# gMLP u products: where the fetches of v, the modulation steps, the first mixing and one PSUM copy stand in the queues

## The chip, the cores and the metric

One core of one Trainium2 chip runs the whole program. The metric is the device time of one execution in microseconds (us), given as the median of several runs. The engines of the core work from queues of their own, in order: PE (TensorE, matmuls, with its weight loads listed as PEld), DVE (VectorE), ACT (ScalarE), POOL (GpSimd, which also issues some transfers) and SP (which only issues transfers). Each waits on semaphores for what another engine or a transfer has finished.

## The reference

Two layers of a hybrid backbone work on 512 latent tokens and 256 context tokens of width 1024, in float32. Each layer is FFN, token mixer, FFN; each part is modulated by vectors made from a conditioning vector and closed by a LayerNorm. The first layer's mixer is the gated MLP that this change touches:

```python
def modulation(cond, w_mod, b_mod):
    m = jax.nn.silu(cond) @ w_mod + b_mod
    return jnp.split(m[..., None, :], N_MOD, axis=-1)

def gmlp_mix(h, w_in, sgu_g, sgu_b, w_s, b_s, w_out):
    b_, t_, _ = h.shape
    u, v = jnp.split(jax.nn.gelu(h @ w_in, approximate=False), 2, axis=-1)
    v = layer_norm(v, sgu_g, sgu_b)
    v = v.reshape(b_, t_ // CHUNK, CHUNK, GMLP_GROUPS, GMLP_HALF // GMLP_GROUPS)
    v = jnp.einsum('gpq,bnqgc->bnpgc', w_s, v) + b_s.T[None, None, :, :, None]
    return (u * v.reshape(b_, t_, GMLP_HALF)) @ w_out
```

u and v are 3072 wide. v is normalised over its width, mixed over each chunk of 128 tokens by a 128x128 matrix per group (8 groups of 384 columns), multiplied with u, and projected back to 1024.

## The kernel before

Every float32 product is made of three fp32r products: an operand is split into a rounded part (a CAST on ACT) and the rest (a subtraction on DVE), and of the four products the smallest is left out. All recorded engine instructions pass through one helper, so most rows name line 90.

**The u products.** `gmlp` (line 1426) first makes v, all of which is written to DRAM (`v_spill`), and then runs a loop over 24 column blocks j of u, two per turn, a = 0, 2, ..., 22. A turn holds seven Strassen products of 12 matmuls, named B11, T1, T2, B21, T3, B22, T4, each over 384 tokens (half of the 768). They share three kinds of PSUM banks: `seeded` (takes a copy of B11's result, then T2, T3 and T4 on top), `b1` (B11, then B21 on top) and `b2` (T1, then B22 on top). Because T3 adds to the bank in which T2's result still has to be read, the copy of T2's bank to SBUF must be done before T3 starts; the bank of T1 in the next turn must have been read by the addition after B22.

**A slot.** After each product `step` (line 1537) calls `slot` (line 181), which writes instructions in this order: the subtractions of the splits that are due (`flush`), an `early` function if one is given, up to two new weight units (`pump`: CASTs on ACT, sums for Strassen on DVE, loads into 6 `raw` buffers on SP as these come free; 8 `w` buffers hold finished units), modulation steps if `fills` is set, and then `post`: the reading of the bank, and up to two pieces of the list `late`. A pass of the program's own scheduling then sets the final order on DVE and ACT; PE, SP and POOL keep the order in which they were written.

**The mixing.** `spatial(j)` (line 1500) multiplies the six normalised 128x128 blocks of v's column block j with the group's matrix into two of four mixing banks that are used in turn. A transposition and a small product of the next group take one bank of the four every third j. `mixed(0)` and `mixed(1)` read the two banks on DVE (three 128-wide blocks each, into `S`), and `times` multiplies `S` with u into `stage`, which POOL writes to DRAM. `fetch(j + 4)` asks SP for the block of v that goes into the ring place that j has just left. For a > 0, `spatial(a)` stands between B21 and T3 and `spatial(a+1)` between B22 and T4; the turn a = 0 does both after T4.

**Modulation steps.** `fill` runs one step of `mod_unit` (line 453): two DVE multiply-adds of a loaded 128x512 piece of w_mod (`mraw`, 3 buffers, loaded on SP) into `acc`; every eighth step ends with two all-reduces over partitions on POOL (line 476) and the next begins with two TENSOR_SCALARs. This sub-layer has 48 steps: 33 in the u loop (T1, B21 and B22 of a = 2 to 20, and T4 of a = 4, 12 and 20), 13 in the first half of the output projection, 2 in its second half.

**The output projection.** `out_proj` (line 884) reads the products back through POOL transfers into `q`, splits them and multiplies them with 24 weight pieces per half of the 1024 columns. In the first seven slots of the second half the six banks of the first half are added to z, one per slot.

Of the kernel before, what the change touches and what calls it, by code (L numbers as in the profile page):

```python
# [94 lines left out]
class Backbone:  # L95
# [788 lines left out]
    def out_proj(self, acts, l, i, factor, end, prev, gate_at=2):  # L884

        self.pin(True)
        n = acts.n
        orders = acts.order
        acts.feed(0, 3)
        self.new_z(NB)  # L890
        residual = []
        st = self.stats(NB)
        banks, adds = {}, []
        for half, order in enumerate(orders):
            body = n - CLOSE * half
            for x in range(body):
                f = order[x]
                (w,) = self.weights(1)
                for b in range(NB):
                    if not x:  # L900
                        if half:
                            z = self.z[b][:, 0:512]
                            adds.append((b, z, self.gated(b, 0, banks[b], factor)))
                            self.unhold(("out", b))
                        banks[b] = self.bank(("out", b))
                    self.products(banks[b], b, [acts.of(f)], [w], x == 0, x == n - 1)
                    if b == 2:
                        self.flush()
                        self.pump(1)
                        acts.prepare(half, x + AHEAD)  # L910
                self.release(1)
                self.flush()
                if not half and x == 1:
                    residual = self.residual(prev, NB)
                if not half and x == gate_at:
                    self.load_gate(l, i + 2, NB)
                if not half or x > 3:
                    acts.feed(half, 3 - half)
                if adds:
                    if x:  # L920
                        b, z, tmp = adds.pop(0)
                        self.dve.tensor_tensor(z, z, tmp, ALU.add)
                        self.dve.bn_stats(st[b][:, 0], z)
                    self.fill(int(prev is None or self.light))
                elif residual and x > 2 and (half or x % 2):
                    residual.pop(0)()
                    self.fill(int(self.light))
                elif half or x < n - 1:
                    self.fill_pair()
                    if prev is None and x % 8 == 3:  # L930
                        self.fill()
        assert not residual
        rest = [acts.of(f) for f in orders[1][n - CLOSE :]]
        ws = self.weights(CLOSE)
        self.flush()
        self.pump()
        self.pin(False)

        def closing(b, between):
            self.products(banks[b], b, rest[:2], ws[:2], False, False)  # L940
            turned = between()
            self.products(banks[b], b, rest[2:], ws[2:], False)
            if b == NB - 1:
                self.release(CLOSE)
                self.pump(1 if end.strassen else 9)

            def add():
                self.add_gated(b, 1, banks[b], factor, st[b])
                self.unhold(("out", b))

            return [add], st[b], turned

        end.run(NB, closing)
# [472 lines left out]
    def gmlp(self, l, i, nblocks, end, prev):  # L1426
# [45 lines left out]
        def fetch(j):  # L1472
            if j < GMLP_CH:
                src = spill[j // 4][:, (j % 4) * P : (j % 4) * P + P].rearrange("(b p) c -> p b c", p=P)
                self.sp.dma_start(ring[:, j % 4], src)
# [18 lines left out]
            dve.scalar_tensor_tensor(nb, mv[:, :, 0], -1.0, self.v_rs, ALU.mult, ALU.mult)  # L1494

        self.following = group(0)
        late = []
        kept = {}

        def spatial(j):  # L1500
            if j % 3 == 0:
                self.grp = self.grp_next
                self.following = group(j // 3 + 1) if j // 3 + 1 < GMLP_GROUPS else iter((None, None, None))
            wT, r, bs = self.grp
            self.grp_next = next(self.following)
            if j % 3 == 2:
                load_ws(j // 3 + 2)
            v = ring[:, j % 4]
            banks = [mix_bank(), mix_bank()]
            for b in range(NB):  # L1510
                o = (b % HALF) * P
                self.mm(banks[b // HALF][:, o : o + P], v[:, b], wT, True, True)
            fetch(j + 4)
            box = []

            def mixed(x):
                if not x:
                    base = self.sm([P], "base", 2)
                    sc = self.sguT[:, GMLP_CH + j : GMLP_CH + j + 1]
                    dve.scalar_tensor_tensor(base, r, sc, bs, ALU.mult, ALU.add)  # L1520
                    box.append(base[:, :].unsqueeze(1).to_broadcast([P, HALF, P]))
                cut = lambda t: t.rearrange("p (b t) -> p b t", t=P)
                out = cut(S[j % 2][:, x * HT : x * HT + HT])
                gain = self.sguT[:, j : j + 1]
                dve.scalar_tensor_tensor(out, cut(banks[x][:, 0:HT]), gain, box[0], ALU.mult, ALU.add)

            late.extend([lambda: mixed(0), lambda: mixed(1)])
# [9 lines left out]
        def step(ps, name, go_on, early, *posts, fills=0):  # L1537
            self.product(ps, name, go_on)

            def post():  # L1540
                for f in posts:
                    f()
                for _ in range(2):
                    if late:
                        late.pop(0)()

            self.slot(post, 2, fills, early)
            self.release(1)

        add = lambda out, a, b: dve.tensor_tensor(out, a, b, ALU.add)  # L1550
# [7 lines left out]
        for a in range(0, GMLP_CH, 2):  # L1558
            begin, final = not a, a == GMLP_CH - 2
            seeded = self.part_bank("mixed", marked=True)  # L1560
            b1, extra = self.part_bank(), int(not begin and a < GMLP_CH - 2)
            step(b1, "B11", False, lambda: act.copy(seeded, b1), v_stats if begin else lambda: normed(a))
            b2, p5 = self.part_bank(), temp()
            step(b2, "T1", False, None, lambda: act.copy(p5, b2), v_bias if begin else nothing, fills=extra)
            if begin:
                next(self.following)
            if final:
                acts.prepare(0, 0)
                acts.feed(0, 1)
            v = temp()  # L1570
            half = (lambda j, x: lambda: normed(j, range(HALF * x, HALF * x + HALF))) if begin else lambda j, x: nothing
            step(seeded, "T2", True, None, lambda: act.copy(v, seeded), half(0, 0))
            g = temp()
            step(b1, "B21", True, None, lambda: gelu(g, b1), half(0, 1), fills=extra)
            if begin:
                self.grp_next = next(self.following)
            else:
                spatial(a)
                late.append(lambda a=a, g=g: times(a, T1, g))
            w = temp()  # L1580
            step(seeded, "T3", True, lambda: act.copy(w, seeded), half(1, 0) if begin else lambda: normed(a + 1))
            if final:
                acts.prepare(0, 1)
                acts.feed(0, 1)
            step(b2, "B22", True, None, lambda: add(v, v, b2), lambda: add(w, w, p5), half(1, 1), fills=extra)
            if begin:
                self.filler_raw()
            else:
                spatial(a + 1)
            if a == GMLP_CH - 4:  # L1590
                acts.feed(0, 1)
            x = temp()

            def last():
                gelu(v, v)
                gelu(w, w)
                gelu(x, seeded)

            step(seeded, "T4", True, None, last, fills=int(extra and a % 8 == 4))
            self.unhold("mixed")  # L1600
            if final:
                acts.prepare(0, 2)
            if begin:
                spatial(a)
                late.append(lambda a=a, g=g: times(a, T1, g))
                late.append(lambda a=a, v=v: times(a, T2, v))
                spatial(a + 1)
            else:
                late.append(lambda a=a, v=v: times(a, T2, v))
            late.append(lambda a=a, x=x: times(a + 1, T1, x))  # L1610
            late.append(lambda a=a, w=w: times(a + 1, T2, w))
# [734 lines left out]
```

## Time and profile before

| what | value |
|---|---|
| median of 3 runs | 2789.63 us (2788.86 to 2789.99) |
| the profiled execution | 2794.73 us, of which the span is 2792.9 us |
| u loop and mixing | from 736.4 us to 966.2 us of the span |
| output projection | from 966.2 us to about 1169 us |
| PE busy over the span | 2735.2 us (98%) |
| mean granted TensorE clock | 0.994 |

The page lists busy times by engine and by group of instructions; the span is from the first to the last instruction of the profiled execution. A timeline row holds a start, a duration, the engine, the operation and, in brackets, how long the engine sat idle before it and what ended that. In a row of windows the number after the engines' busy times is the clock that the throttle granted to PE in that stretch, 1.00 being full speed. SPq rows are transfers issued by SP. A merged row (x6) covers several instructions.

### The profile page before, as it was taken

Reading aid. Unit: us, or ns where it says so; the run is one execution under the profiler, and the core shown is the slowest. Engines: PE = TensorE matmul, PEld = TensorE weight load, DVE = VectorE, ACT = ScalarE, POOL = GpSimd, SP = SyncE. Lnnn points to the kernel's source line nnn. Section 1 sums busy time; section 2 is a strip of 40 time slices with the busy share of each in tenths; the row PEclk is TensorE's granted clock in tenths of the full one; section 3 lists DMA queues with packets and bytes.
Section 4 is the critical chain, followed back from the end, with each engine's and each line's share of the span. In section 5 each row is a group of like instructions: output and inputs, shape, how many; then the busy total and the mean of one; then the engine's idle time right before and its main releaser. Section 6 shows DMA issues by size and latency. Waiting matters only on the chain.

```text
span 2792.9 us, 40728 instructions
## 1 busy us (share of the span) xinstructions
PE 2735.2 (98%) x14234; PEld 2464.5 (88%) x14234; DVE 2085.0 (75%) x3554; ACT 1313.8 (47%) x2624; POOL 554.2 (20%) x627
## 2 busy tenths in 40 slices
PE   7999999999999999999999999999999999999998
PEld 5999987887899988899998889999888888888887
DVE  6879979586789876587898659789796698733445
ACT  6544432475656632564444246444432666623321
POOL 1002144212123231200314120013242121000001
PEclk9999999999999999999999999999999999999999
DMA  7445466367666683444456534454594424454352
GB/s 234 134 140 144 142 225 213 110 212 226 201 187 184 190 271 105 132 147 147 136 147 224 169 105 146 139 151 137 174 309 147 147 72 90 132 149 130 111 170 87
DMA packets 408134, 448.09 MB, mean 160 GB/s; under 512 B 29624, under 2 KB 289144, under 8 KB 407928
## 3 DMA queue, kind: packets, MB, share of 16 engines
q1 hardware_dynamic: 371416, 331.99, 38.5%
q0 software_dynamic: 36512, 113.51, 13.4%
q8 instruction: 111, 1.82, 0.3%
q14 instruction: 95, 0.78, 0.1%
HBM read 383.40 MB, written 64.19 MB: 160 GB/s over the span
## 4 chain that ended last, share of the span: by engine, by line
PE 58%; DVE 2%; ACT 2%; issue 2%; POOL 1%; DMA 1%; SPq 0%; DVEq 0%; POOLq 0%; ACTq 0%
PE ps L90 57%; PE pp L90 1%; POOL acc L476 1%; ACT h L694 0%; ACT z L2244 0%; POOL rs L204 0%; ACT p L1758 0%; DMA mraw<-in_w_mod_dram 0%; DMA q<-act 0%; DVE z L90 0%; DVE nm L1750 0%; DVE w L90 0%; ACT w L173 0%; ACT comb L708 0%; DVE q L90 0%
## 5 line engine op out<-in xcount | busy, mean ns | idle before, releaser
L90 PE MATMUL ps<-comb,w 128*128 128x384 f32 x6552 | 1155.4, 336 | 11.7 <-ACT q L90 4.4
L90 PEld LDWEIGHTS ps<-comb,w 128*128 128x128 f32 x6552 | 1139.5, 189 | 17.1 <-ACT q L90 5.5
L90 PE MATMUL ps<-w,acts 128*128 128x512 f32 (+1 forms) x3792 | 864.8, 390 | 7.1 <-DVE q L90 5.1
L90 PEld LDWEIGHTS ps<-w,acts 128*128 128x128 f32 x3792 | 709.2, 188 | 154.6 <-DVE q L90 6.0
L90 ACT CAST w<-raw 128x512 fp32r<-128x512 f32 x643 | 397.8, 622 | 638.9 <-PE ps L90 547.6
L90 DVE TENSOR_TENSOR w<-raw,w 128x512 fp32r<-128x512 f32 x643 | 476.8, 746 | 291.1 <-ACT w L90 289.7
L90 DVE SCALAR_TENSOR_TENSOR acc<-mraw,cs,acc 128x512 f32<-128x512 f32 x392 | 279.8, 745 | 26.2 <-DMA mraw<-in_w_mod_dram 25.9
L476 POOL PARTITION_ALL_REDUCE acc<-acc x56 | 206.5, 3693 | 326.8 <-DVE acc L90 306.6
L90 PE MATMUL ps<-h,w 128*128 128x512 f32 (+1 forms) x1152 | 241.4, 372 | 0.2 <-DVE w L174 0.2
L90 PEld LDWEIGHTS ps<-h,w 128*128 128x128 f32 x1152 | 203.3, 188 | 37.7 <-DVE w L174 0.4
L90 POOL DMA_DIRECT2D act<-stage x86 | 49.7, 578 | 878.1 <-DVE stage L90 791.7
L90 POOL DMA_DIRECT2D q<-act x234 | 132.4, 603 | 450.8 <-DVE acts L90 276.7
L90 ACT COPY q<-ps 128x384 f32<-128x384 f32 (+1 forms) x218 | 104.7, 480 | 228.2 <-PE ps L90 228.1
L90 DVE TENSOR_TENSOR w<-sums,w 128x512 fp32r<-128x512 f32 x234 | 166.9, 721 | 45.6 <-ACT w L90 45.4
L90 PE MATMUL ps<-w,comb 128*128 128x512 f32 x756 | 173.7, 390 | 2.5 <-ACT ps L90 2.0
L90 ACT CAST w<-sums 128x512 fp32r<-128x512 f32 x234 | 144.9, 620 | 64.1 <-DVE sums L339 39.2
L90 PEld LDWEIGHTS ps<-w,comb 128*128 128x128 f32 x756 | 141.3, 188 | 33.5 <-ACT ps L90 2.9
L90 ACT CAST acts<-q 128x384 fp32r<-128x384 f32 (+1 forms) x272 | 131.9, 519 | 66.9 <-DMA q<-act 48.8
L90 DVE TENSOR_TENSOR acts<-q,acts 128x384 fp32r<-128x384 f32 (+1 forms) x272 | 153.7, 602 | 12.2 <-ACT acts L90 12.2
L204 POOL TENSOR_TENSOR rs<-ve,mhalf 128x1 f32<-128x1 f32 (+3 forms) x47 | 38.6, 820 | 273.6 <-DVE ve L201 170.7
L90 DVE TENSOR_TENSOR q<-q,ps 128x384 f32<-128x384 f32 (+1 forms) x81 | 46.1, 570 | 57.7 <-PE ps L90 57.6
L174 DVE TENSOR_TENSOR w<-raw,w 128x512 fp32r<-128x512 f32 x101 | 67.2, 688 | 25.6 <-ACT w L173 25.1
(203 smaller groups left out, 2484.3 us busy)
## 6 DMA issues: line engine op xcount, KB each, us to landing
raw<-in_ffn_w_in_dram SPq DMA_DIRECT2D x400, 256.0 KB
mraw<-in_w_mod_dram SPq DMA_DIRECT2D x256, 256.0 KB
raw<-in_ffn_w_out_dram SPq DMA_DIRECT2D x176, 256.0 KB
q<-act POOLq DMA_DIRECT2D x224, 192.0 KB, 4.3
raw<-in_gmlp_w_in_dram SPq DMA_DIRECT2D x132, 256.0 KB
act<-stage POOLq DMA_DIRECT2D x76, 384.0 KB, 3.2
zhat<-z POOLq DMA_DIRECT2D x26, 512.0 KB, 3.0
raw<-in_gmlp_w_out_dram SPq DMA_DIRECT2D x48, 256.0 KB
```

The costliest lines, as they stand in the source:

```text
L90: return self.tc.keep_in_program_order(f(*args, **kwargs))
L174: self.lows.append((key, lambda: self.dve.tensor_tensor(lo, src, hi.bitcast(F32), ALU.subtract)))
L204: self.last_rstd = self.nc.gpsimd.tensor_tensor(rs, ve, self.mhalf[:, 0:1].to_broadcast([P, n]), ALU.pow).ins
L476: nc.gpsimd.partition_all_reduce(accs[c], accs[c], P, bass_isa.ReduceOp.add)
```

## The change

Five edits, all in the mixer of the first layer:

1. `fetch(j + 4)` is no longer issued at once by `spatial(j)`. It goes on a list with a counter of 2, which every later `step` lowers, and is issued at the end of the second one.
2. Modulation steps in the u loop start at a = 4 and leave T4 out: 27 in place of 33 (T1, B21 and B22 of a = 4 to 20). `step` hands 0 to `slot` and calls `fill_pair` itself, behind `post` and behind the fetches. The first three loads of `mraw` move from a = 0 to the end of B22 of a = 2. In the output projection of this mixer (`acts.ring`), the seven slots at the start of the second half run a step each, which they did not before.
3. T2's copy out of `seeded` becomes the slot's `early` function, written ahead of the weight CASTs.
4. In the turn a = 0, the two `mixed` of j = 0 are called as soon as `spatial(0)` is written, not two slots later.
5. The conditions around these are rewritten to fit.

```diff
@@ out_proj
-                    self.fill(int(prev is None or self.light))
+                    self.fill(int(prev is None or self.light or acts.ring))
@@ gmlp
-        late = []
+        late, fetches = [], []
...
-            fetch(j + 4)
+            fetches.append([2, j + 4])
...
-            self.slot(post, 2, fills, early)
+            self.slot(post, 2, 0, early)
+            for x in fetches:
+                x[0] -= 1
+            while fetches and fetches[0][0] <= 0:
+                fetch(fetches.pop(0)[1])
+            if fills:
+                self.fill_pair()
             self.release(1)
...
-            b1, extra = self.part_bank(), int(not begin and a < GMLP_CH - 2)
+            b1, extra = self.part_bank(), int(3 < a < GMLP_CH - 2)
...
-            step(seeded, "T2", True, None, lambda: act.copy(v, seeded), half(0, 0))
+            step(seeded, "T2", True, lambda: act.copy(v, seeded), half(0, 0))
...
-            if begin:
+            if not begin:
+                spatial(a + 1)
+            if a == 2:
                 self.filler_raw()
-            else:
-                spatial(a + 1)
...
-            step(seeded, "T4", True, None, last, fills=int(extra and a % 8 == 4))
+            step(seeded, "T4", True, None, last, fills=0)
...
             if begin:
                 spatial(a)
+                for _ in range(2):
+                    late.pop(0)()
                 late.append(lambda a=a, g=g: times(a, T1, g))
```

On ACT, in the slots of T1, T2 and B21 of one turn (the last six blocks of v normalised, then `w<-sums` and `w<-raw` as weight CASTs, `q<-ps` as copies out of PSUM, the last row being the gelu after B21):

```order
 L90 ACTIVATE v<-v,v_nb,rs_7221 128x128 x6
 L90 CAST w<-sums 128x512
-L90 COPY q<-ps 128x384
-L90 CAST w<-sums 128x512
-L90 COPY q<-ps 128x384
+L90 COPY q<-ps 128x384 x2
+L90 CAST w<-sums 128x512
 L90 CAST w<-raw 128x512
 L90 ACTIVATE q<-ps 128x384
```

The second copy, which is T2's, now follows T1's copy directly, and the second CAST of a sum has gone behind it; this holds in the turns a = 2 to 20 (in a = 22 two CASTs of the output projection's first operand stand between the copies).

On DVE, at the end of the turn a = 0, with the numbers of the buffers (`ps_7369` of before and `ps_7363` of the change are the first mixing bank of j = 0, `S_7185` the mixed result, `s512` the row that is added to it). Before:

```order
L90 TENSOR_TENSOR w_7332<-sums_7239,w_7332 128x512
L339 TENSOR_TENSOR sums_7435<-sums_7434,raw_7126 128x512
L90 TENSOR_TENSOR w_7361<-raw_7106,w_7361 128x512
L90 SCALAR_TENSOR_TENSOR s512_7415<-S_7185,sguT_82 128x128
L90 TENSOR_SCALAR acc_7442<-mraw_7341,cs_78 128x512
L90 SCALAR_TENSOR_TENSOR S_7185<-ps_7369,sguT_82,s512_7415 128x384
```

and with the change:

```order
L90 TENSOR_TENSOR w_7332<-sums_7239,w_7332 128x512
L90 SCALAR_TENSOR_TENSOR s512_7371<-S_7185,sguT_82 128x128
L90 SCALAR_TENSOR_TENSOR s512_7436<-S_7185,sguT_82 128x128
L339 TENSOR_TENSOR sums_7431<-sums_7430,raw_7126 128x512
L90 SCALAR_TENSOR_TENSOR S_7185<-ps_7363,sguT_82,s512_7371 128x384
```

Between the same subtraction for a weight and the reading of the first mixing bank there were four operations, one of them a modulation step's; now there are three, two of them 128 wide.

On POOL, from the turn a = 18 to the last (`act<-stage` are the products written to DRAM, L476 the all-reduces of modulation, L477 their transfers, `q<-act` the first product read back for the output projection):

```order
 L90 DMA act_18_7181<-stage 128x768
 L90 DMA act_19_7182<-stage 128x768
-L476 ISA acc<-acc 128x512
-L477 DMA mod_8467<-acc 16x1x32
-L476 ISA acc<-acc 128x512
-L477 DMA mod_8467<-acc 16x1x32
 L90 DMA q<-act_0_7163 128x384 x2
-L90 DMA mod_9427<-in_b_mod_dram 16x64 x2
 L90 DMA act_20_7183<-stage 128x768
 L90 DMA act_21_7184<-stage 128x768
```

A pair of all-reduces that stood ahead of the first reading back has left this place. Over the u loop POOL had four such pairs and now has three.

## The prediction

> **What bounds the kernel now.** The page first:
>
> ```profile
> span 2792.9 us, 40728 instructions
> PE 2735.2 (98%) x14234; PEld 2464.5 (88%) x14234; DVE 2085.0 (75%) x3554; ACT 1313.8 (47%) x2624; POOL 554.2 (20%) x627
> PE 58%; DVE 2%; ACT 2%; issue 2%; POOL 1%; DMA 1%; SPq 0%; DVEq 0%; POOLq 0%; ACTq 0%
> ```
>
> PE is busy for 98% of the span and leads the chain of waits, so edits that leave the matmuls alone can only win where PE stands still. The PE timeline of the u loop shows where (start, duration, in brackets the idle time ahead and what ended it):
>
> ```profile
> 756.84 1.62 PE L90 MATMUL ps<-zraw,v 128*128 128x128 f32 x6 [3.22 <-DVE S L90]
> 811.07 0.91 PE L90 MATMUL ps<-zraw,v 128*128 128x128 f32 x6 [0.96 <-DVE S L90]
> 817.92 8.09 PE L90 MATMUL ps<-comb,w 128*128 128x384 f32 x36 [1.76 <-DVE q L90]
> 864.08 4.43 PE L90 MATMUL ps<-comb,w 128*128 128x384 f32 x24 [0.81 <-ACT q L90]
> 883.64 4.43 PE L90 MATMUL ps<-comb,w 128*128 128x384 f32 x24 [1.27 <-ACT q L90]
> 903.62 4.46 PE L90 MATMUL ps<-comb,w 128*128 128x384 f32 x24 [1.80 <-ACT q L90]
> 958.03 4.45 PE L90 MATMUL ps<-comb,w 128*128 128x384 f32 x24 [0.51 <-ACT q L90]
> 970.49 36.60 PE L90 MATMUL ps<-w,acts 128*128 128x512 f32 x153 [2.02 <-ACT q L90]
> ```
>
> Eight gaps, 12.35 us. Three cost more than their length. The windows right behind the first, third and last, and for contrast behind the sixth (third figure from the end: granted clock):
>
> ```profile
> 756.00:761.00 5.00, 4.16 (x17) 4.19 (x18) 3.95 (x9) 0.00 (x0) 0.57 (x1) 0.66 0.76 212
> 818.00:822.00 4.00, 4.00 (x14) 4.00 (x15) 4.00 (x9) 4.00 (x10) 0.00 (x0) 0.57 0.35 95
> 971.00:976.00 5.00, 5.00 (x16) 3.93 (x16) 5.00 (x11) 2.84 (x6) 2.43 (x5) 0.66 0.51 151
> 903.00:908.00 5.00, 4.38 (x25) 4.38 (x26) 5.00 (x11) 3.55 (x10) 1.18 (x2) 1.00 0.51 158
> ```
>
> A window of 5 us at 0.66 loses 5 x 0.34 = 1.7 us of matmul time, one of 4 us at 0.57 4 x 0.43 = 1.7. So three gaps have a clock loss of 1.7 us each behind them, and 12.35 + 5.1 = 17.5 us is all that can be won here, 0.6% of the span.
>
> **First mixing (edit 4): 3.6 us.** In the turn a = 0 `spatial(1)` needs, for its second bank, the bank of `mixed(0)` of j = 0. DVE before that gap:
>
> ```profile
> 752.39 0.68 DVE L90 TENSOR_TENSOR w<-sums,w 128x512 fp32r<-128x512 f32 x1
> 753.11 0.69 DVE L339 TENSOR_TENSOR sums<-sums,raw 128x512 f32<-128x512 f32 x1
> 754.32 0.34 DVE L90 SCALAR_TENSOR_TENSOR s<-S,sguT 128x128 f32<-128x128 f32 x1
> 755.68 0.49 DVE L90 TENSOR_SCALAR acc<-mraw,cs 128x512 f32<-128x512 f32 x1 [1.02 <-DMA mraw<-in_w_mod_dram]
> 756.08 1.14 DVE L90 SCALAR_TENSOR_TENSOR S<-ps,sguT,s 128x384 f32<-128x384 f32 x2
> ```
>
> A modulation step with a late `mraw` stands in front of the reading (756.08, the first of two 0.57 long; PE goes on at 756.84). In the new order the same subtraction is followed by two 128-wide operations, L339 and then the reading: 752.39 + 0.6 + 2 x 0.3 + 0.65 = 754.2 as its start (each start follows the last by a little less than its duration), its end at 754.8, PE on at 755.0. PE stopped at 753.62 (756.84 - 3.22), so 1.3 us of gap stay and 1.9 go. If nothing came of it 0, if all went 3.2. I also count the 1.7 of clock, because gaps of 1.27 and 1.80 us above had x24 at full rate behind them (4.43 and 4.46 us): 3.6. It is not sure, since length alone doesn't decide: 1.76 us lost the clock, 1.80 did not (rival 1).
>
> [...]
>
> **T2's copy (edit 3): 4.4 us.** The four gaps that end with "ACT q" ahead of x24 stand in front of T3. One of them, at 903.62:
>
> ```profile
> 898.98 3.49 POOL L476 PARTITION_ALL_REDUCE acc<-acc  x1
> 899.19 2.69 DVE L90 TENSOR_TENSOR stage<-q,S 128x384 f32<-128x384 f32 x1
> 901.80 0.68 DVE L339 TENSOR_TENSOR sums<-sums,raw 128x512 f32<-128x512 f32 x1
> 902.57 0.62 ACT L90 CAST w<-sums 128x512 fp32r<-128x512 f32 x1 [4.20 <-DVE sums L339]
> 903.09 0.47 ACT L90 COPY q<-ps 128x384 f32<-128x384 f32 x1
> ```
>
> ACT stood 4.20 us for the sum, with T2's copy behind it. The copy now goes first; T2 ends one product (about 2.1 us, 12 of the x24 in 4.43) and a spatial ahead of T3, and the copy takes 0.47, so it is covered. Behind it now wait the CAST of the sum and, through it, B21's gelu and T3's copy; the weights are several slots ahead, and T3's copy has the length of B22 and a spatial, some 4 us, as cover. All four go: 0.81 + 1.27 + 1.80 + 0.51 = 4.39; from below 0, if the next ACT wait takes their place.
>
> **Fewer steps, behind the slot's work (edit 2): 4.4 us at a = 6.** What led to the second and third gap:
>
> ```profile
> 802.79 5.87 POOL L476 PARTITION_ALL_REDUCE acc<-acc  x1
> 805.48 3.45 DVE L90 TENSOR_SCALAR acc<-mraw,cs 128x512 f32<-128x512 f32 x2
> 810.29 3.48 SPq L90 DMA_DIRECT2D raw<-in_gmlp_w_in_dram  x3
> 816.71 0.69 DVE L336 TENSOR_TENSOR sums<-raw 128x512 f32<-128x512 f32 x1 [3.33 <-DMA raw<-in_gmlp_w_in_dram]
> 817.32 0.55 DVE L90 TENSOR_TENSOR q<-q,ps 128x384 f32<-128x384 f32 x1
> ```
>
> While an all-reduce runs, a DVE operation that comes in its later part is held (3.45 us here for two that take 0.5 each, 2.69 for one of 0.55 above). Here the pair of all-reduces was issued by step 8 in T1 of a = 6 and step 9 ran into it. That made the mixing late (0.96), then SP's loads, then L336, behind which the addition waited that frees T1's bank (1.76, and 1.7 of clock). Counted from a = 4, step 8 is B21 of a = 8, step 16 T1 of a = 14, step 24 B22 of a = 18: none falls into a = 6, 12 or 18 ahead of their mixing, the turns in which a transposition takes a mixing bank and the next spatial waits as at a = 0. The additions also stand ahead of the step now. So 4.4 (0 to 4.4).
>
> The six steps that leave are 6 x 2 multiply-adds of 0.745 us, 8.9 us of DVE, and one all-reduce pair. Seven steps go into the output projection's second half:
>
> ```profile
> L90 DVE SCALAR_TENSOR_TENSOR acc<-mraw,cs,acc 128x512 f32<-128x512 f32 x56 | 40.2, 745 | 0.0
> 1077.55 0.69 DVE L90 TENSOR_TENSOR w<-raw,w 128x512 fp32r<-128x512 f32 x1 [2.06 <-ACT w L90]
> 1081.62 0.69 DVE L90 TENSOR_TENSOR w<-raw,w 128x512 fp32r<-128x512 f32 x1 [2.05 <-ACT w L90]
> ```
>
> A slot there lasts 1081.62 - 1077.55 = 4.07 us and DVE idles 2.05 of it; a step's 1.49 fits, so nothing; without that cover 7 x 1.49 = 10.4. Their seven `mraw` loads queue on SP among 256 KB weight loads that are a few slots early. The all-reduces of steps 32, 40 and 48 run on POOL ahead of readings back that are three slots early; the two pairs of before did so without a PE gap.
>
> **The last gap: 1.5 us.** It hangs on a chain through POOL:
>
> ```profile
> 948.77 3.47 POOL L476 PARTITION_ALL_REDUCE acc<-acc  x1
> 957.47 1.09 POOL L90 DMA_DIRECT2D q<-act  x2
> 964.92 0.51 ACT L90 CAST acts<-q 128x384 fp32r<-128x384 f32 x1 [1.16 <-DMA q<-act]
> 965.65 0.51 ACT L90 CAST acts<-q 128x384 fp32r<-128x384 f32 x1 [0.22 <-DMA q<-act]
> 966.67 0.55 DVE L90 TENSOR_TENSOR q<-q,ps 128x384 f32<-128x384 f32 x1
> 969.97 0.47 ACT L90 ACTIVATE q<-ps 128x384 f32<-128x384 f32 x1
> ```
>
> The reading back lands late, its splitting precedes the additions on DVE, these precede the gelus, and the last gelu frees a bank that the output projection wants. The pair of all-reduces at a = 20, behind which POOL and DVE stood until about 952.5, is gone from there, so the reading can be issued some us sooner; ACT then saves its 1.16 and 0.22 of waiting, leaving 2.02 - 1.4 = 0.6 and perhaps no clock loss: 3.1. But the transfer took 7.5 us to land and what held it I can't see, so half: 1.5 (0 to 3.7).
>
> **Fetches of v (edit 1): nothing.** In place of S or w_s, v, three raw loads, SP issues the raw loads first and v behind them; a later v load also passes one modulation load. v is wanted two turns on (a turn is 20 us by the rows 883.64 and 903.62), which covers two products. The raw loads come forward by one v issue, about 0.4 us, and DVE waits for them:
>
> ```profile
> DVE sums L336 <- DMA raw<-in_gmlp_w_in_dram: 15.2, 9, 3.3
> ```
>
> (15.2 us in nine waits, the longest 3.3.) Only the longest reached PE, so 0; up to the 3.5 of that one, which is counted above.
>
> For gaps that I have not found I put back 1.1, the mean of the four copies' gaps. 3.6 + 4.4 + 4.4 + 1.5 - 1.1 = **12.8 us**. The profiled execution took 2794.73 (span 2792.9 and 1.8 around it), 5.1 more than the median; I take the gain off the median: 2789.63 - 12.8 = **2776.8**. Its own bounds: 2772.2 if all 17.4 go, 2784 where under half does.
>
> **Rivals.** 1. *The stalls come half back.* Step 16 in T1 and step 17 in B21 of a = 14 is the pattern of a = 6, and could cost 4.4 again; and the 1.3 us left at 755 could still lose the clock, 1.7. Against it: a = 16 had the same pattern before and only T2's copy waited. 12.8 - 6.1 = 6.7 us of gain: 2782.9.
> 2. *Only the copies help.* DVE is busy for most of the loop; if it is late for reasons other than the steps, the other gaps reappear one product later, and 4.4 us remain: 2785.2. For it: three of eight gaps end with DVE. Against: the removed 8.9 us of DVE work and one pair's hold.
> 3. *Raw loads become the bound (slower).* SP's refill of `mraw` waits for the step's multiply-adds, which now stand behind the slot's additions; the next raw load waits behind that refill on SP, L336 on the load, the addition and T1's bank on L336. A wait of 3.33 at L336 gave a 1.76 gap, so it tells from about 1.6 us on. If the refill comes 1.4 later (a step's length), the mean wait of 15.2 / 9 = 1.7 becomes 3.1, and each of the nine turns with steps has 1.5 of gap and 1.7 of clock: 9 x 3.2 = 29 us, less 12.8: 2806. It decides from four or five turns on. Against it: the step was in front of the same load before, and ends only one slot's work later.
>
> **Numbers.** Forecast 0.62, rival 1 0.16, rival 2 0.14, rival 3 0.08. Range 2772 to 2787: all of the gain at one end, past rival 2 at the other. A difference of 0.2% (5.6 us) is about what a measurement can tell, so forecast and rival 1 are faster (0.78), rival 2 the same (0.14), rival 3 slower (0.08).
>
> **What would show it.** Right: no PE gap ended by ACT q ahead of a x24; a gap of 1 to 1.5 us, at full clock, at about 755; none near 811 to 818; all-reduce pairs at a = 8, 14 and 18; PE without idle in the output projection's second half with DVE under 4 us a slot. Wrong: half clock behind 755; L336 waiting over 1.6 us in several turns; gaps in front of T1 or behind 1064.

## The result, and the profile after

The change takes 2782.36 us (median of 8 runs, 2778.78 to 2784.98) where the kernel before takes 2789.24 beside it (8 runs, 2785.13 to 2793.55). The ratio is 0.9972, 95% interval 0.9962 to 0.9983: 7.8 us faster by the ratio, 4.7 to 10.6, and 6.9 by the medians. The forecast was 12.8. The time is inside the predicted range and on the predicted side, but the gain is about half of the forecast, and near that of rival 1 (6.7).

The profiled execution of the change took 2782.34 us. The page's first lines:

```profile
span 2780.6 us, 40722 instructions
PE 2728.8 (98%) x14234; PEld 2460.8 (89%) x14234; DVE 2082.2 (75%) x3554; ACT 1314.7 (47%) x2624; POOL 554.4 (20%) x627
```

The PE timeline of the u loop after the change, rows with idle time ahead of them (in brackets, with what ended it):

```profile
753.68 0.91 PE L90 MATMUL ps<-zraw,v 128*128 128x128 f32 x6 [1.99 <-DVE S L90]
876.78 0.91 PE L90 MATMUL ps<-zraw,v 128*128 128x128 f32 x6 [0.40 <-DVE S L90]
883.52 6.52 PE L90 MATMUL ps<-comb,w 128*128 128x384 f32 x36 [1.66 <-DVE q L90]
933.15 1.26 PE L90 MATMUL ps<-zraw,v 128*128 128x128 f32 x6 [1.76 <-ACT v L90]
935.19 1.62 PE L90 MATMUL ps<-zraw,v 128*128 128x128 f32 x6 [0.78 <-DVE S L90]
961.25 83.92 PE L90 MATMUL ps<-w,acts 128*128 128x512 f32 x369 [0.48 <-ACT q L90]
```

Six gaps, 7.07 us, where there were eight with 12.35. The four in front of T3 and the two of a = 6 are gone, and the last one is 0.48. But four of the six are new: two at a = 14 (876, and 883, which stands in front of T1 of the next turn) and two at a = 20 (933 and 935). The windows over them (third figure from the end: granted clock):

```profile
753.00:758.00 5.00, 4.32 (x27) 4.35 (x28) 4.83 (x11) 1.28 (x3) 0.71 (x2) 1.00 0.36 96
883.00:887.00 4.00, 3.48 (x20) 3.48 (x21) 4.00 (x8) 3.50 (x9) 0.00 (x0) 1.00 0.63 177
932.00:937.00 5.00, 3.07 (x14) 2.73 (x15) 5.00 (x11) 2.94 (x7) 0.66 (x2) 0.73 0.99 330
937.00:942.00 5.00, 5.00 (x19) 5.00 (x18) 4.90 (x10) 2.55 (x5) 0.00 (x0) 0.59 0.61 188
```

Only a = 20 lost clock here: the x60 behind its gaps (five products in one row) took 12.82 us where the loop's others take 10.7, and the second mixing 1.62 in place of 0.91, 2.8 us together. What made its gaps, from the timeline of all engines:

```profile
920.48 4.26 POOL L476 PARTITION_ALL_REDUCE acc<-acc  x1 [11.11 <-DVE acc L90]
921.56 2.33 DVE L90 SCALAR_TENSOR_TENSOR s<-S,sguT 128x128 f32<-128x128 f32 x1
925.47 3.18 DVE L90 TENSOR_TENSOR w<-raw,w 128x512 fp32r<-128x512 f32 x1
925.64 3.46 POOL L476 PARTITION_ALL_REDUCE acc<-acc  x1
930.58 0.87 DVE L90 TENSOR_SCALAR acc<-mraw,cs 128x512 f32<-128x512 f32 x2
931.38 0.68 DVE L347 TENSOR_TENSOR raw<-raw 128x512 f32<-128x512 f32 x1
932.09 0.62 ACT L90 CAST w<-raw 128x512 fp32r<-128x512 f32 x1 [2.26 <-DVE raw L347]
932.61 2.41 ACT L90 ACTIVATE v<-v,v_nb,rs 128x128 f32<-128x128 f32 x6
```

The all-reduces are those of step 24, issued in B22 of a = 18, as counted. They hold one DVE operation each (2.33 for a 128-wide one that took 0.34 in the prediction's rows, 3.18 for one that takes 0.69), about 4.5 us together. DVE therefore comes late to L347 of a = 20, ACT waits 2.26 us for it with a CAST, and the normalising of v, for which PE waits, stands behind that CAST.

Two sections with the same work in every kernel make the comparison firmer than single gaps. The u loop is measured from the first small product (`ident,s`) of the mixing part, at about 740, to the first `w,acts` product; the output projection from there to the `comb` product of the next part that follows a wait of 0.5 us for w in every kernel (at 1180.37 before). The u loop went from 225.6 to 220.0 us, the output projection from 214.2 to 211.0 (the last gap and its clock loss lie in it). That is 8.8 of the 12.4 us by which the two profiled executions differ. The rest lies outside the edits: 2.1 ahead of the mixing part, 1.4 behind it.

### The profile page after: what moved, and what is told of

Its sections match the earlier page's. It is cut to its first block, busy times and chain, and to the rows that moved or that the text cites. A ratio compares the mean times of both kernels' runs of the same rounds, so it can differ in the third digit from the quotient of the medians.

```text
span 2780.6 us, 40722 instructions
## 1 busy us (share of the span) xinstructions
PE 2728.8 (98%) x14234; PEld 2460.8 (89%) x14234; DVE 2082.2 (75%) x3554; ACT 1314.7 (47%) x2624; POOL 554.4 (20%) x627
## 4 chain that ended last, share of the span: by engine, by line
PE 77%; DVE 7%; issue 5%; DMA 4%; ACT 4%; POOL 2%; SPq 0%; DVEq 0%; ACTq 0%; POOLq 0%
PE ps L90 77%; DVE w L90 1%; DMA mraw<-in_w_mod_dram 1%; DVE acc L90 1%; POOL acc L476 1%; PE pp L90 1%; ACT w L90 1%; DMA raw<-in_w_mod_dram 1%; DMA q<-act 1%; DMA acc<-in_gmlp_w_in_dram 1%; DMA raw<-in_gmlp_w_in_dram 1%; ACT h L694 1%; ACT z L2252 0%; POOL q L90 0%; DVE z L90 0%
## 5 line engine op out<-in xcount | busy, mean ns | idle before, releaser
L90 PEld LDWEIGHTS ps<-comb,w 128*128 128x128 f32 x6552 | 1139.1, 189 | 10.1 <-DVE w L90 3.8
L476 POOL PARTITION_ALL_REDUCE acc<-acc x56 | 206.6, 3697 | 324.3 <-DVE acc L90 297.1
L90 DVE TENSOR_TENSOR acts<-q,acts 128x384 fp32r<-128x384 f32 (+1 forms) x272 | 153.6, 602 | 11.1 <-ACT acts L90 11.0
```

The costliest lines, as they stand in the source:

```text
L90: return self.tc.keep_in_program_order(f(*args, **kwargs))
L476: nc.gpsimd.partition_all_reduce(accs[c], accs[c], P, bass_isa.ReduceOp.add)
```

## The experiments

Ten kernels, and the change and the kernel before once more, each run beside the kernel before on the same chip. Sections and gaps are of the one profiled execution of each:

| kernel | median, us | ratio to before, 95% | u loop, us | PE gaps up to the last one, us |
|---|---|---|---|---|
| before | see above | | 225.6 | 12.35 |
| before again | 2788.26 | one run | 223.4 | 11.44 |
| change | 2782.36 | 0.9972 (0.9962 to 0.9983) | 220.0 | 7.07 |
| change again | 2781.46 | 0.9973 (0.9962 to 0.9984) | 217.2 | 7.09 |
| copy only | 2790.66 | 1.0002 (0.9993 to 1.0012) | 226.4 | 10.47 |
| mixing only | 2787.58 | 0.9991 (0.9981 to 1.0) | 223.0 | 10.49 |
| steps only | 2786.02 | 0.9987 (0.9978 to 0.9996) | 223.1 | 8.32 |
| fetches only | 2787.23 | 0.9988 (0.9979 to 0.9997) | 224.8 | 11.28 |
| change without copy | 2782.3 | 0.997 (0.9959 to 0.9981) | 220.1 | 6.39 |
| change with fetch at once | 2778.99 | 0.9959 (0.9944 to 0.9974) | 215.2 | 4.40 |
| change without all-reduces | 2775.45 | 0.9947 (0.9932 to 0.9962) | 211.5 | 1.89 |
| other phase | 2775.56 | 0.9949 (0.9932 to 0.9966) | 213.3 | 3.03 |
| other phase, fetch at once | 2776.4 | 0.9954 (0.9942 to 0.9966) | 213.3 | 2.83 |
| same, mixing earlier | 2775.53 | 0.9954 (0.9942 to 0.9965) | 212.0 | 1.50 |

### Each edit alone

**The copy.**

```diff
-            step(seeded, "T2", True, None, lambda: act.copy(v, seeded), half(0, 0))
+            step(seeded, "T2", True, lambda: act.copy(v, seeded), half(0, 0))
```

> Before, with T2's copy written as the slot's early function and nothing else. Theory A (each edit acts at its own place): the four gaps ended by ACT ahead of T3 go, 0.81 + 1.27 + 1.80 + 0.51 = 4.4 us, the other four stay (3.2, 0.96, 1.76, 2.02) with their clock losses: time about 4.4 us below before. Rival B (DVE's load decides where PE stands): ACT waits for the sums as long as before, only further on, and gaps of the same sum come back ahead of B21's readers: time within 1 us of before.

No difference (1.0002). The gaps in front of T3 went, all but one of 2.48 at a = 22; others came. Around a = 14, from the timeline:

```profile
876.95 0.68 DVE L339 TENSOR_TENSOR sums<-sums,raw 128x512 f32<-128x512 f32 x1
877.67 0.62 ACT L90 CAST w<-sums 128x512 fp32r<-128x512 f32 x1 [5.84 <-DVE sums L339]
879.98 2.44 ACT L90 ACTIVATE v<-v,v_nb,rs 128x128 f32<-128x128 f32 x6
880.54 2.42 PE L90 MATMUL ps<-zraw,v 128*128 128x128 f32 x12 [1.47 <-ACT v L90]
```

ACT waits for the same sum as before (5.84 here). T2's copy no longer stands behind it, but the normalising of v does, and PE now stops for v, at the mixing that stands just ahead of T3. Rival B's outcome.

**The first mixing.**

```diff
                 spatial(a)
+                for _ in range(2):
+                    late.pop(0)()
```

> Before, with the two readings of the first mixing called as soon as it is written (a = 0) and nothing else. Theory A: the gap at about 756 shrinks from 3.22 to 1.3 (as predicted) or to the 1.99 that the change has left, with the clock kept behind it: 2.9 to 3.6 us below before; the other seven gaps as before. If the 1.99 of the change comes from T2's earlier copy in the turn a = 0, the gap is near 1.3 here; if it comes from the engines' general state there, it is near 2.0. Rival B: the reading waits for other DVE work and the gap stays over 3: no difference.

```profile
752.38 0.91 PE L90 MATMUL ps<-zraw,v 128*128 128x128 f32 x6 [1.23 <-DVE S L90]
752.00:757.00 5.00, 4.62 (x29) 4.65 (x30) 4.15 (x10) 1.57 (x4) 1.17 (x3) 1.00 0.54 184
```

The gap is 1.23 at full clock (first row from the PE timeline, second from the windows), against a predicted 1.3. The u loop is 2.7 us shorter than in the first profile of before (0.4 than in the second) and the median 3.0 lower, an interval that still touches no change.

**The steps.** The condition of the count, the place of the steps, the first loads of `mraw` and the seven slots of the output projection, as in the diff of the change.

> Before, with 27 modulation steps in the u loop from a = 4 on, behind the slot's work, and seven in the output projection's second half, and nothing else. Theory A (what counts is in which slot the all-reduces fall): the gaps of a = 6 (0.96 and 1.76 with 1.7 of clock) and the last one (2.02 with 1.7 of clock, to about 0.5) go, 7.6 us; at a = 14 and a = 20 new gaps come, as in the change (0.40 + 1.66, and 1.76 + 0.78 with about 2.2 of clock: 6.8 us); T2's gaps and the first mixing's stay. Sum: 0.8 below before, 0 to 3. Rival B (less DVE work in the loop is what helps, 8.9 us less): T2's four gaps shrink as well, and no gap comes at a = 14 or a = 20: 7 to 12 below before.

2786.02, 4.6 us below before by the medians (1.1 to 6.1 by the interval). Its largest gaps in the PE timeline:

```profile
753.71 0.93 PE L90 MATMUL ps<-zraw,v 128*128 128x128 f32 x6 [2.44 <-DVE S L90]
917.00 0.91 PE L90 MATMUL ps<-zraw,v 128*128 128x128 f32 x6 [1.32 <-ACT w L90]
932.86 7.17 PE L90 MATMUL ps<-comb,w 128*128 128x384 f32 x24 [2.96 <-ACT q L90]
```

Neither theory had it whole. The gaps of a = 6 went, as theory A has it; T2's four gaps went too without the copy, as rival B has it; and a new gap came in front of T3 at a = 20, where there was none before, with the clock at 0.50 behind it (932 to 937). The gaps in front of T3 were thus a sign of DVE being late, not of the copy's place.

**The fetches.**

```diff
-            fetch(j + 4)
+            fetches.append([2, j + 4])
```

with the counter's loop behind the slot.

> Before, with the fetches of v issued two products later and nothing else. Theory A: nothing, within 1 us of before, the eight gaps at their places. Rival C (the order on SP matters): DVE's wait for raw loads at L336 changes by more than 3 us in sum from 15.2, or the gap at a = 6 (1.76, ended by the addition behind such a wait) changes by over 1 us, or a wait for v by the normalising appears: 1 to 4 us to either side.

2787.23, 3.4 us below (0.8 to 5.9). The gaps of a = 6 shrank to one of 0.34 (start 813.01), two of those in front of T3 grew to 2.30 and 2.46 (starts 878.49 and 899.15) and that of a = 22 to 1.36 (start 954.36). The prediction took the order on SP to be neutral; the gaps did move. Where the gain lies the profile doesn't show: the u loop is 0.8 us shorter than in the first profile of before and 1.4 longer than in the second, and the last gap, 0.47, differs between executions of one kernel too (2.02 and 1.33 before).

### Taking parts out of the change

**Without the copy.** The reverse of the first diff.

> The change without its edit 3: T2's copy stands behind the weight CASTs again, all else as changed. Theory A of the prediction (the copies are worth 4.4 on their own): gaps in front of T3 come back, 4 us or more over the change, about 2786 to 2787. Theory D, from the first four runs (the copy alone only moved ACT's wait for the sum on to the normalising of v, and the steps alone took T2's gaps away): no gap in front of T3 but the one at a = 20, which comes as 2.9 us with half clock behind it, as it did with the steps alone, in place of 1.76 + 0.78; the first mixing's gap, 1.99 in the change, is 1.2 to 1.3 as with edit 4 alone if the copy of a = 0 made the difference. Time within 2 us of the change, 2781 to 2784.

2782.3, the time of the change. The gaps of before do not come back in front of T3. What is left lies elsewhere again:

```profile
753.31 1.34 PE L90 MATMUL ps<-zraw,v 128*128 128x128 f32 x6 [1.99 <-DVE S L90]
881.42 1.62 PE L90 MATMUL ps<-zraw,v 128*128 128x128 f32 x6 [3.55 <-DVE S L90]
```

Theory D had the time right and the place wrong: a = 14 has the large gap here, and a = 20 almost none (0.37). The scheduling has put L355 ahead of the small copy out of the mixing bank at a = 14; it is L355 that the second all-reduce holds (2.72 us from 878.36 for an operation of 0.69; the pair runs from 872.79 to 881.52), the copy comes at 881.00, and PE goes on at 881.42.

The first mixing's 1.99 stays without the copy, so the copy is not what made it 1.99 in place of 1.23. DVE's first wait for a raw load in the loop, of the change and, below it, of the kernel with the first mixing alone, shows what did:

```profile
748.32 0.69 DVE L336 TENSOR_TENSOR sums<-raw 128x512 f32<-128x512 f32 x1 [2.33 <-DMA raw<-in_gmlp_w_in_dram]
747.28 0.69 DVE L336 TENSOR_TENSOR sums<-raw 128x512 f32<-128x512 f32 x1 [2.76 <-DMA raw<-in_gmlp_w_in_dram]
```

Counted from the first small product (738.55 and 738.11), L336 starts after 9.77 us in the change and after 9.17 with the mixing alone. The reading of the bank then starts 4.60 behind L336 in the change (752.92) and 4.34 in the other (751.62), where one 128-wide operation fewer stands between. The two differences account for the 0.8 us. In seven profiles, the change's two, the one without the copy and four of the kernels below, the distance is 4.6, and the gap goes with the start of L336: 1.10 at 8.77 us, 1.34 at 9.00, 1.41 at 9.06, 1.81 at 9.46, 1.90 at 9.56, 1.99 at 9.77 and at 9.83.

**With the fetches at once.**

```diff
-            fetches.append([2, j + 4])
+            fetch(j + 4)
```

> The change without its edit 1: v is fetched at once by each mixing, all else as changed. Prediction (edit 1 is worth nothing): the gaps of the change at their places, within 1 us of it. Theory E (edit 1 brings the raw loads forward, as alone it took the gap at a = 6 from 1.76 to 0.34): DVE's wait for raw loads grows and a gap ended by the addition comes back at one of a = 6, 12 or 14; 2 to 4 us over the change, about 2785.

2778.99: not slower but lower by 3.4 us, though the intervals of the two overlap. Theory E is refuted in its sign. On the same chip the change without the copy took 2780.93 to 2784.10, all above the highest run here (2780.08). The u loop is 2 to 5 us shorter than in the two profiles of the change. The gaps at a = 14 (2.06) are gone, those at a = 20 shrank from 2.54 to 0.54 and the first mixing's to 1.34, while 0.44 + 0.29 came at a = 16 and 1.31 at a = 18. At a = 14 the pair of step 16 and the operations that it holds, from the timeline of all engines:

```profile
867.10 9.33 POOL L476 PARTITION_ALL_REDUCE acc<-acc  x2
869.88 3.47 DVE L90 TENSOR_SCALAR acc<-mraw,cs 128x512 f32<-128x512 f32 x2
870.94 4.41 PE L90 MATMUL ps<-comb,w 128*128 128x384 f32 x24
873.46 2.52 DVE L90 TENSOR_TENSOR w<-raw,w 128x512 fp32r<-128x512 f32 x1
```

It starts 3.84 us ahead of T3's product (870.94, merged with B22's) here. The change's pair of that turn started at 870.80, 0.50 ahead of T3's product at 871.30. The same hold costs PE nothing when DVE is 3.3 us further ahead. Less waiting may be part of it: at L336 DVE waited ten times for raw loads of this mixer's weights in the change, 18.6 us in all, and seven times here, 11.1 us. The order that the scheduling gives DVE also differs in this kernel, and which of the two puts DVE ahead was not separated.

**Without the all-reduces.**

```diff
-                nc.gpsimd.partition_all_reduce(accs[c], accs[c], P, bass_isa.ReduceOp.add)
+                if not self.skip_reduce:
+                    nc.gpsimd.partition_all_reduce(accs[c], accs[c], P, bass_isa.ReduceOp.add)
```

`skip_reduce` is set during the u loop only.

> The change with the all-reduces over partitions of this sub-layer's modulation left out (the multiply-adds and the transfers stay; the modulation of the next sub-layer is therefore wrong, the amount of other work the same). Theory D (the new stalls at a = 14 and a = 20 come from DVE operations that are held while an all-reduce runs on POOL): the gaps 0.40 + 1.66 at a = 14 and 1.76 + 0.78 with 2.2 of lost clock at a = 20 go, nothing comes in their place; the first mixing's 1.99 stays: 6 to 7 us below the change, about 2776. Rival (DVE is late there by its own work, or by late raw loads): the gaps stay within 1 us of what they are in the change.

2775.45, as theory D gave it. Two gaps are left in the u loop:

```profile
751.64 0.91 PE L90 MATMUL ps<-zraw,v 128*128 128x128 f32 x6 [1.41 <-DVE S L90]
951.48 83.96 PE L90 MATMUL ps<-w,acts 128*128 128x512 f32 x369 [0.48 <-ACT q L90]
```

The multiply-adds, their loads and the late fetches are all still there, and at both turns DVE runs the same operations in the same order as in the change. At a = 14 the change had (the first row from POOL)

```profile
870.80 8.73 POOL L476 PARTITION_ALL_REDUCE acc<-acc  x2
872.98 3.47 DVE L90 TENSOR_SCALAR acc<-mraw,cs 128x512 f32<-128x512 f32 x2
876.56 2.52 DVE L90 TENSOR_TENSOR w<-raw,w 128x512 fp32r<-128x512 f32 x1
```

and this kernel, for the same two DVE operations,

```profile
869.94 0.89 DVE L90 TENSOR_SCALAR acc<-mraw,cs 128x512 f32<-128x512 f32 x2
870.93 0.69 DVE L90 TENSOR_TENSOR w<-raw,w 128x512 fp32r<-128x512 f32 x1
```

The stalls at a = 14 and a = 20 are the all-reduces'. This shows the cause, not how a held operation is held.

DVE's waits at L336 are eleven here, 23.1 us in all, the longest 4.3; in the change they were ten, 18.6 and 4.6. So the kernel without these stalls waits longer for its raw loads. A DVE that is early waits, and in the u loop of this kernel such a wait costs PE nothing, except for the first, behind which the gap of the first mixing stands.

### Moving the all-reduces

**Other phase.** Four steps fewer in the u loop, so that step 16 comes into B21 of a = 14 and step 24 into the output projection:

```diff
-            step(b1, "B21", True, None, lambda: gelu(g, b1), half(0, 1), fills=extra)
+            step(b1, "B21", True, None, lambda: gelu(g, b1), half(0, 1), fills=extra and a < GMLP_CH - 4)
...
-            step(b2, "B22", True, None, lambda: add(v, v, b2), lambda: add(w, w, p5), half(1, 1), fills=extra)
+            step(b2, "B22", True, None, lambda: add(v, v, b2), lambda: add(w, w, p5), half(1, 1), fills=extra and a not in (12, 16, 20))
```

> The change with four steps fewer in the u loop (no step at B22 of a = 12, 16 and 20 nor at B21 of a = 20; the output projection takes them), so that the pairs of all-reduces fall into B21 of a = 8 and B21 of a = 14, and the third into the output projection. Theory D (the place of the all-reduces decides): no gap at a = 20; at a = 14 none as at a = 8 in the change; about 6.8 below the change, 2775.5. Rival: in B21 of a = 14 the hold makes the sum at T3's copy late, 1 to 2 us of gap stay there: 2777 to 2778. Rival F (four steps' DVE work, 6 us, is what helps): the gaps of both turns shrink in proportion, by a seventh: 2781.

2775.56, where theory D gave 2775.5. From the timeline of all engines, the larger gaps in the loop and what stands ahead of them:

```profile
749.16 0.91 PE L90 MATMUL ps<-zraw,v 128*128 128x128 f32 x6 [1.10 <-DVE S L90]
859.21 0.69 DVE L336 TENSOR_TENSOR sums<-raw 128x512 f32<-128x512 f32 x1 [3.27 <-DMA raw<-in_gmlp_w_in_dram]
860.42 6.54 PE L90 MATMUL ps<-comb,w 128*128 128x384 f32 x36 [0.92 <-DVE q L90]
870.33 3.66 POOL L476 PARTITION_ALL_REDUCE acc<-acc  x1 [3.06 <-DVE acc L90]
871.00 2.54 DVE L90 TENSOR_TENSOR w<-raw,w 128x512 fp32r<-128x512 f32 x1
875.57 2.32 DVE L90 TENSOR_TENSOR w<-raw,w 128x512 fp32r<-128x512 f32 x1
879.00 6.52 PE L90 MATMUL ps<-comb,w 128*128 128x384 f32 x36 [0.32 <-DVE q L90]
```

The pair still holds DVE (2.54 and 2.32 for operations of 0.69), and 0.32 of it reaches PE. The 0.92 ends with the addition behind L336, which had waited 3.27 for a raw load. Nothing is lost at a = 20. The third pair now runs in the output projection, which takes 211.0 us as in the change. The four steps are 6 us less DVE work in the loop as well, and one pair fewer. Rival F, by which that work is what helps, gave 2781, and the kernel without all-reduces kept the work and had still fewer gaps, so the work alone does not make the stalls. How much the lighter DVE adds at a = 14, where the pair comes two products later, was not separated from the new place.

**Other phase with the fetches at once**, by the diff shown above.

> The kernel with the all-reduces at B21 of a = 8 and of a = 14 alone, and the fetches of v at once as before the change. Theory E (the late fetches cost the change 3 us): the 0.21 + 0.92 + 0.32 that are left at a = 8, 12 and 14 of that kernel go, 2773.5 to 2774.5. Rival H (the fetches only matter where an all-reduce falls into T1, a = 14 of the change): within 1 us of 2775.5.

2776.4, u loop 213.3 in both: nothing, as rival H has it. In these kernels late fetches cost something only together with the pair at T1 of a = 14.

**The same with the first mixing a product earlier.**

```diff
-            if not begin:
-                spatial(a + 1)
+            spatial(a if begin else a + 1)
...
             if begin:
-                spatial(a)
-                for _ in range(2):
-                    late.pop(0)()
```

> As the kernel with the phase and the fetches, with the mixing of j = 0 written behind B22 of a = 0 instead of behind T4, and its readings in T4's slot. The first mixing's gap (1.1 to 2.0 in the other kernels) goes, since a product of 2.1 us stands between the two mixings: 1.1 to 1.4 us less than the kernel without it. Rival: the reading is late by DVE's other work there, and the gap stays or moves in front of T4's bank: no difference.

```profile
754.98 0.91 PE L90 MATMUL ps<-zraw,v 128*128 128x128 f32 x6 [1.01 <-DVE S L90]
```

The gap is 1.01 where the kernel without it had 1.81: smaller, but neither gone nor unchanged, so neither expectation holds. The reading starts 3.99 us behind L336 in place of 4.60, which is most of the difference. The u loop is 1.35 us shorter, the medians differ by 0.9, which can't be told from no change. These last three kernels lie 5 to 7 us below the change by the medians, and 4 to 8 us by the u loop (212.0 to 213.3 against 217.2 to 220.0); the intervals of the ratios touch or overlap slightly. Two of the three ran on the same chip as the change's second series, and there no runs overlap: 2778.95 to 2783.52 for the change, 2773.43 to 2778.45 for the two.

### The same kernels again

> The change itself once more, to see which of its gaps stay from one execution to the next. Theory D (the gaps at a = 14 and a = 20 are made by the all-reduces' places): gaps at both turns again, 4 to 6 us in sum with their clock losses, the first mixing's between 1.2 and 2.0; 2780 to 2783. Rival G (the gaps wander by chance): the sum is the same but the gaps stand at other turns, or one of the two turns has none.

The gaps stand at the same places with the same sum (1.90, 0.85, 1.66, 1.42, 0.78 and 0.48: 7.09 against 7.07), so rival G falls. Yet the u loop is 2.8 us shorter. The windows around a = 20:

```profile
930.00:935.00 5.00, 2.79 (x18) 2.23 (x17) 5.00 (x10) 2.94 (x7) 1.15 (x3) 1.00 1.02 341
935.00:940.00 5.00, 5.00 (x30) 5.00 (x29) 4.99 (x10) 3.62 (x8) 0.00 (x0) 1.00 0.60 209
```

The clock was 1.00 in both, where the first execution had 0.73 and 0.59 behind gaps of the same kind.

> The kernel before once more, with its profile. The prediction took the last gap (2.02, with 1.7 of lost clock) as standing; in the kernels that alter only T2's copy, only the first mixing or only the fetches it was 0.32, 1.20 and 0.47, with the clock kept. If it wanders, it is 0.3 to 1.2 here and its 3.2 us were no part of the median of before; if it stands, 2 with half clock. The gaps of a = 0, of a = 6 and in front of T3 stay within 1 us each.

```profile
754.99 0.91 PE L90 MATMUL ps<-zraw,v 128*128 128x128 f32 x6 [3.14 <-DVE S L90]
803.70 6.00 PE L90 MATMUL ps<-comb,w 128*128 128x384 f32 x24 [2.29 <-ACT q L90]
965.77 34.99 PE L90 MATMUL ps<-w,acts 128*128 128x512 f32 x153 [1.33 <-ACT q L90]
```

The gaps in front of T3 at the later turns stand (0.89, 1.33, 1.62 and 0.84). The first mixing's stands too, but with the clock at 1.00 behind it this time, where it was 0.66 in the first profile. At a = 6 the pair shows as one gap of 2.29 in front of T3, with the clock at 0.66 behind it, in place of 0.96 and 1.76. The last gap is 1.33 at full clock: of the 3.7 us that I put on it (2.02 and 1.7 of clock), 2.4 were of that one execution.

## Why the prediction was right, and where not

The gain came out near rival 1's 6.7, but by luck: of the two things that rival 1 names, the first mixing kept its clock and a = 14 cost half of what it says, and the rest came from a = 20, which it doesn't name. The base of the sum was also one execution's. Gaps and clock losses of the two profiles of before are 17.4 and 13.1 us (11.44, and 1.7 of clock at a = 6), those of the change 9.9 (7.07 and 2.8) and 7.1. The means differ by 6.8, which is what the medians show.

**First mixing (3.6).** The working held: 1.23 of gap with this edit alone against 1.3, though with one 128-wide operation fewer ahead of the reading than it counted. In the change 1.99 and 1.90 are left: L336, which waits for a raw load ahead of all that the prediction added up, starts 9.77 us behind the first small product in place of 8.92 (749.52 in the profile of before). The 1.7 of clock was counted in full, though called not sure. The clock behind this gap was lost in four of the five profiles without the edit and in one of the nine with it (by the windows, or by the x48 behind it, 8.6 us at full clock and 9.5 to 10.1 after a loss), so it was worth about 0.7 x 1.7 = 1.2.

**T2's copy (4.4).** This step failed, in its cause. The four gaps did go in the change, but the copy alone gained nothing, taking it out of the change cost nothing, and the steps alone took all four away. The prediction had this outcome in its own lower bound ("from below 0, if the next ACT wait takes their place") and chose the upper end. What it overlooked is that B21's readers and T3's copy, whose cover it worked out, are not all that waits behind the CAST of the sum: the normalising of v does too, and PE needs it for the mixing ahead of T3.

**Fewer steps, behind the slot's work (4.4).** Right for a = 6 (0.96 + 1.76 + 1.7; nothing is left there), and this edit also carried the copy's 4.4. The sentence that let the new places off was wrong: "none falls into a = 6, 12 or 18 ahead of their mixing". Those turns are not what decides. At all three turns of the change the pair holds DVE for 3.5 to 4.5 us (by the operations that take longer than elsewhere), and whoever next needed DVE paid unless DVE was ahead. At a = 8 it cost nothing, at a = 14 0.40 + 1.66 (0.85 + 1.66), at a = 20 1.76 + 0.78 with 2.8 of clock (1.42 + 0.78 without). Rival 1 named a = 14 at 4.4 with its clock; 2.1 to 2.5 came. a = 20 was in no rival. Together 4.7 to 7.4 us, in place of the 1.1 put back for gaps not found; 5 to 6 are missing from the 12.8.

**The last gap (1.5).** 0.48 is left. From the two profiles of before 0.9 to 3.2 was gained, within the bounds given. That the pair at a = 20 caused it is not shown: it was also 0.32 and 0.47 in kernels that keep the pair there.

**The fetches (0).** The zero does not hold in general. Alone the late fetches gained 3.4 us (0.8 to 5.9), in the change they cost perhaps 3, where DVE comes to the pair of a = 14 later than without them, and with the other phase nothing. The mechanism behind the gain is open.

**Output projection (0 for seven steps).** Right: 211.0 us from its first product to the next part, the same with seven more steps, with eleven and with a third pair, and no PE gap in it but the 0.48 at its start.

**Rivals 2 and 3.** Rival 2's premise, DVE late for other reasons than the steps, fell with the steps-only kernel. Rival 3 took a wait at L336 of over 1.6 us as a gap to come; in the change the longest, 4.6, had no gap behind it, and the kernel without all-reduces waited most there and had none but the first mixing's and the last. So the sign that the prediction gave for it, waits of over 1.6 us at L336 in several turns, did come (five of the ten in the change: 2.33, 4.57, 2.18, 1.80 and 2.11) and told little. Its mechanism exists at a small size: 0.92 behind a wait of 3.27 in the kernel with the other phase, and the part of the first mixing's gap that goes with the landing of the load.

## What to carry to other kernels

When several gaps of the main engine end with different engines, look first for one event that makes them all late (here POOL's all-reduces holding DVE); moving the instruction that is last in each chain can just pass the wait to the next one, as moving T2's copy did here (ratio 1.0002). A periodic piece of work that is thinned out can keep its cost per event (here each pair of all-reduces that was left in the loop held DVE for 3.5 to 4.5 us): list where each event lands in the new count, and price every landing as the old ones, not only those that look alike. Before a gap goes into a sum of a few microseconds, see it in a second profile of the same kernel.

## What the runs showed of the hardware

**In these profiles the gap's length did not decide the clock loss behind it.** Behind 1.99 the clock was 1.00 in the change and 0.66 in the change without the copy; this row is from the windows of the latter:

```profile
752.00:757.00 5.00, 3.69 (x14) 3.72 (x15) 5.00 (x11) 0.01 (x1) 0.59 (x1) 0.66 0.33 80
```

Two executions of one kernel also came out differently. Behind the first mixing's gap it was 1.00 after 3.14 us in the second profile of before and 0.66 after 3.22 us in the first. At a = 20 it was 0.73 and 0.59 in one profile of the change and 1.00 in the other, behind 1.76 + 0.78 and 1.42 + 0.78 us. What decides it these runs don't show.

**The all-reduces over partitions held some DVE operations and not others.** Held were, among others, `w<-raw,w` (2.54 and 3.18 in place of 0.69), `s<-S,sguT` (2.33 in place of 0.34) and the pair of TENSOR_SCALARs (3.47 in place of 0.87). The prediction says that it is an operation in the later part of an all-reduce that is held; the rows show no such rule, for the 2.69 of its own rows began 0.21 us behind the start of an all-reduce (898.98) and the 2.33 of the change 1.08 behind one (920.48). Nor was every operation held that met one: in the pair that begins at 870.80 in the change, L347 at 871.17 took its 0.69 and two `w<-sums,w` from 871.77 took 1.30 together, before the first was held at 872.98. What decides which one is held was not shown.
